# Rolling the rows of a matrix: the head columns loaded as four whole pieces per partition, with the row ends passed on inside SBUF

## The chip, the cores and the metric

The kernel runs on one core of a Trainium2 chip. The core has compute engines, of which this kernel uses two: VectorE (DVE in the profile) for copies inside the on-chip memory SBUF, and GpSimd (POOL), here only to issue DMAs. Two more, SyncE (SP) and ScalarE (ACT), also only issue DMAs. All DMAs of a core are executed by the same 16 DMA engines, whichever engine issued them; the profile calls SP's queue q1 or q10, ACT's the other of these, and POOL's q0. SBUF has 128 partitions. The big arrays lie in DRAM (HBM).

The metric is device time in microseconds; lower is better. Before the change three runs gave 816.09, 816.27 and 818.35 us, median 816.27.

## The reference

```python
def reference(x, shift):           # x: 8192 x 8192 float32, shift: 100
    return np.roll(x, shift, axis=1)
```

Each row is rotated by 100 columns: `out[r, 100:] = x[r, :8092]` and `out[r, :100] = x[r, 8092:]`. Nothing is calculated; 268 MB are read and 268 MB are written. A row is 32 KB.

## The kernel before

The work is cut by columns at `a = 256`. With `s = 100` (the shift) and `g = a - s = 156`:

- **The body**, columns 256 to 8191 of the output, is a plain copy from DRAM to DRAM with the columns shifted by 100. It is issued from SP and ACT (lines 34 to 46), SP going through the rows from the top and ACT from the bottom. One DMA takes 16 rows (every fourth of 64), 496 KB, so each DMA engine has one row of 31 KB; the last two blocks of each side are cut in two by columns. That is 264 DMAs from each of SP and ACT. The name of the last DMA of each block is kept in `marks`.
- **The head**, columns 0 to 255 of the output, goes through SBUF and is issued from POOL. The rows are taken in 16 stages of 512 rows; in a stage each of the 128 partitions has four consecutive rows, q = 0 to 3. A stage has a tile `t` into which DRAM is read and a tile `h` of 128 x 4 x 256 which is written out by one DMA of 512 KB (line 94).

What makes the head cheap to read is that the array is contiguous: the 256 elements that start 100 before the start of row r are the wrapped end of row r-1 (100 elements) followed by the first 156 elements of row r. Such a run of 1 KB is called a piece here. Its first 100 elements belong in the output's row r-1, its last 156 in row r. Before the change a stage reads three pieces per partition, those that start rows q = 1, 2 and 3 (line 85). They give the ends for rows 0, 1, 2 and the starts for rows 1, 2, 3. The two parts that are left, the end of row 3 (400 B per partition, line 86) and the start of row 0 (624 B per partition, line 89), are read straight into `h`. VectorE copies the other parts from `t` to `h` (lines 87 and 90).

What sets the order: POOL works through its instructions in order, first the 48 reads of all stages, then the 16 writes. The helper `fetch` (lines 72 to 78) makes each read wait for the read four before it, so at most four are under way. Write k waits for one of the body's DMAs, chosen by `marks` so that the writes are spread from 3/8 to 15/16 of the body (lines 92 to 97). There are as many `t` and `h` tiles as stages, so no buffer is reused. Dependencies between tiles (a copy after the read of its tile, a write after all that fills its tile) become waits automatically.

Of the kernel before, what the change touches and what calls it, by code (L numbers as in the profile page):

```python
# [1 line left out]

# [4 lines left out]


@with_exitstack
def kernel(  # L10
    ctx: ExitStack,
    tc: tile.TileContext,
    x: bass.AP,
    shift: int,
    out: bass.AP,
):
    nc = tc.nc
    n_rows, n_cols = x.shape
    s = shift % n_cols
    a = -(-s // 128) * 128  # L20
    if 0 < a <= 384 and a + 128 <= n_cols:
        a += 128
    g = a - s
    P = nc.NUM_PARTITIONS
    engines = [nc.sync, nc.scalar]
    n_chunks = 16
    rows = n_rows // n_chunks

    xm = x.rearrange("(c e j) w -> c j e w", e=16, j=4)
    om = out.rearrange("(c e j) w -> c j e w", e=16, j=4)
    marks = []
    if a < n_cols:
        blocks = n_rows // 64
        mid = (a + n_cols) // 256 * 128
        for i in range(blocks // 2):  # L40
            parts = ((a, mid), (mid, n_cols)) if i >= blocks // 2 - 2 and a < mid else ((a, n_cols),)
            for j in range(4):
                for eng, c, q in ((engines[0], i, j), (engines[1], blocks - 1 - i, 3 - j)):
                    for lo, hi in parts:
                        ins = eng.dma_start(out=om[c, q, :, lo:hi], in_=xm[c, q, :, lo - s:hi - s])  # L45
            marks.append(getattr(ins, "ins", ins).name)
    if a == 0:
        return


    if a > 512:
        for i in range(n_chunks):
            r = slice(i * rows, (i + 1) * rows)
            nc.gpsimd.dma_start(out=out[r, :s], in_=x[r, n_cols - s:])
            if g > 0:
                nc.gpsimd.dma_start(out=out[r, s:a], in_=x[r, :g])
        return

    Q = 4
    n_st = n_rows // (P * Q)
    reads = ctx.enter_context(tc.tile_pool(name="reads", bufs=n_st))
    heads = ctx.enter_context(tc.tile_pool(name="heads", bufs=n_st))
    xt = x.rearrange("(k p q) c -> k p q c", q=Q, p=P)
    ot = out.rearrange("(k p q) c -> k p q c", q=Q, p=P)
    tiles = []
    chain = []  # L70

    def fetch(to, of):
        ins = nc.gpsimd.dma_start(out=to, in_=of, single_packet=True)  # L73
        ins = getattr(ins, "ins", ins)
        if len(chain) >= 4:
            tc.add_manual_dep(ins, chain[-4].name,
                              mybir.DependencyInfo(mybir.DependencyClass.Sync, mybir.DependencyReason.DATA))
        chain.append(ins)

    for k in range(n_st):  # L80
        t = reads.tile([P, Q - 1, a], x.dtype)
        h = heads.tile([P, Q, a], x.dtype)
        lead = bass.AP(tensor=x.tensor, offset=(k * P * Q + 1) * n_cols - s,
                       ap=[[Q * n_cols, P], [n_cols, Q - 1], [1, a]])
        fetch(t[:], lead)
        fetch(h[:, Q - 1, :s], xt[k, :, Q - 1, n_cols - s:])
        nc.vector.tensor_copy(h[:, :Q - 1, :s], t[:, :, :s])  # L87
        if g > 0:
            fetch(h[:, 0, s:], xt[k, :, 0, :g])
            nc.vector.tensor_copy(h[:, 1:, s:], t[:, :, s:])  # L90
        tiles.append(h)
    first, last = len(marks) * 3 // 8, len(marks) * 15 // 16
    for k, h in enumerate(tiles):
        ins = nc.gpsimd.dma_start(out=ot[k, :, :, :a], in_=h[:], single_packet=True)  # L94
        if marks and n_st > 1:
            tc.add_manual_dep(getattr(ins, "ins", ins), marks[first + (last - first) * k // (n_st - 1)],
                              mybir.DependencyInfo(mybir.DependencyClass.Sync, mybir.DependencyReason.DATA))


# [1 line left out]
_INS = ['x', 'shift']  # L101
_OUTS = [((8192, 8192), 'float32')]

_NUMBERS = {'shift': 100}


# [26 lines left out]
```

## Time and profile before

| what | value |
|---|---|
| median of three runs | 816.27 us |
| the profiled execution's own time | 816.2 us |
| its span | 814.4 us |
| DVE busy | 12.0 us, 32 instructions |
| POOL busy | 41.2 us, 68 instructions |
| bytes moved by the DMA engines | 276.90 MB, 340 GB/s |
| HBM read / written | 268.44 MB / 268.44 MB, 659 GB/s together |
| median from issue to landing: read of `t` | 29.5 us |
| the two small reads into `h` (78 KB, 50 KB) | 24.3 us, 21.2 us |
| the write of `h` | 21.1 us |
| a body DMA of 496 KB | 12.7 us |

A byte copied from DRAM to DRAM counts once in the bytes moved and twice in the HBM traffic. The share of a DMA queue is the time that its packets took, as a part of the time of all 16 DMA engines. A packet is the unit in which the profile records what one DMA engine does for one queue; small packets include the completion record that each DMA leaves on each engine.

### The profile page before, as it was taken

The numbers are of one execution on the slowest core, as the hardware profiler recorded it, in microseconds if no ns is written. First come the engines' busy times: TensorE is split into PE (matmuls) and PEld (weight loads), VectorE is DVE, ScalarE is ACT, GpSimd is POOL, SyncE is SP. The second block draws the span as 40 slices with busy tenths as digits, with TensorE's granted clock in tenths as the row PEclk, the third lists the DMA queues.
The fourth block names the chain that finished last, engine by engine and source line by source line (L and its number), as shares of the span: only waits on it lengthen the run. The fifth ranks groups of instructions, "written<-read, shape, count | busy, mean of one in ns | idle before, by whom it ended". The sixth has DMA issues, their size and how long they took to land.

```text
span 814.4 us, 689 instructions
## 1 busy us (share of the span) xinstructions
DVE 12.0 (1%) x32; POOL 41.2 (5%) x68
## 2 busy tenths in 40 slices
DVE  0000000000000000000000000000000000000000
POOL 1001001101001000000000000000000000000000
DMA  9999999999999999999999999999999999999998
GB/s 314 346 347 343 351 344 332 338 347 342 356 344 349 345 334 338 345 337 342 337 350 322 352 338 335 357 342 331 352 352 318 356 347 335 340 339 347 334 331 294
DMA packets 22277, 276.90 MB, mean 340 GB/s; under 512 B 9472, under 2 KB 9728, under 8 KB 13824
## 3 DMA queue, kind: packets, MB, share of 16 engines
q1 hardware_dynamic: 8448, 130.04, 46.8%
q10 hardware_dynamic: 8448, 130.04, 44.1%
q0 software_dynamic: 5376, 16.78, 8.1%
q14 instruction: 5, 0.04, 0.0%
HBM read 268.44 MB, written 268.44 MB: 659 GB/s over the span
## 4 chain that ended last, share of the span: by engine, by line
DMA 95%; ACTq 0%; issue 0%; POOLq 0%
DMA out_dram<-in_x_dram 95%; ACTq L45 0%; POOLq L128 0%; POOLq L94 0%
## 5 line engine op out<-in xcount | busy, mean ns | idle before, releaser
L94 POOL DMA_DIRECT2D out_dram<-h x16 | 11.4, 715 | 486.7 <-DMA out_dram<-in_x_dram 448.9
L73 POOL DMA_DIRECT2D h<-in_x_dram x32 | 17.5, 547 | 197.1 <-DMA t<-in_x_dram 165.0
L73 POOL DMA_DIRECT2D t<-in_x_dram x16 | 12.1, 759 | 54.9 <-DMA h<-in_x_dram 54.0
L87 DVE COPY h<-t 128x300 f32<-128x300 f32 x16 | 5.9, 367 | 287.3 <-DMA t<-in_x_dram 287.3
L90 DVE COPY h<-t 128x468 f32<-128x468 f32 x16 | 7.5, 468 | 0.0
L114 POOL MEMSET const-float32-0.0<- 128x1 f32 x1 | 0.1, 99 | 0.2 <-issue 0.2
L114 POOL MEMSET const-bfloat16-1.0<- 128x1 bf16 x1 | 0.1, 102 | 0.0
L114 POOL MEMSET const-float32-1.0<- 128x1 f32 x1 | 0.1, 99 | 0.0
L114 POOL MEMSET const-uint8-127<- 128x1 uint8 x1 | 0.1, 99 | 0.0
## 6 DMA issues: line engine op xcount, KB each, us to landing
out_dram<-in_x_dram SPq DMA_DIRECT2D x248, 496.0 KB, 12.7
out_dram<-in_x_dram ACTq DMA_DIRECT2D x248, 496.0 KB, 12.7
out_dram<-h POOLq DMA_DIRECT2D x16, 512.0 KB, 21.1
t<-in_x_dram POOLq DMA_DIRECT2D x16, 384.0 KB, 29.5
out_dram<-in_x_dram SPq DMA_DIRECT2D x16, 248.0 KB, 5.9
out_dram<-in_x_dram ACTq DMA_DIRECT2D x16, 248.0 KB, 5.9
h<-in_x_dram POOLq DMA_DIRECT2D x16, 78.0 KB, 24.3
h<-in_x_dram POOLq DMA_DIRECT2D x16, 50.0 KB, 21.2
```

Source lines behind the costliest of these rows:

```text
L73: ins = nc.gpsimd.dma_start(out=to, in_=of, single_packet=True)
L87: nc.vector.tensor_copy(h[:, :Q - 1, :s], t[:, :, :s])
L90: nc.vector.tensor_copy(h[:, 1:, s:], t[:, :, s:])
L94: ins = nc.gpsimd.dma_start(out=ot[k, :, :, :a], in_=h[:], single_packet=True)
L114: nc = _bacc.Bacc("TRN2", target_bir_lowering=False, num_devices=1)
```

## The change

A stage now reads all four pieces per partition, those that start rows q = 0 to 3, by one DMA of 512 KB into a tile `t` of 128 x 4 x 256. That gives the ends for rows 0, 1, 2 and the starts of all four rows. The piece q = 0 of partition p+1 begins with the end of row 3 of partition p, so the missing ends are handed over inside SBUF: `pass_on` copies the first 100 elements of piece 0 from partitions 1 to 127 of `t` to partitions 0 to 126 of `h` by a DMA (127 x 400 B), and reads the one end that is left, that of the last partition, from DRAM (400 B). `pass_on` for stage k-2 is issued after the read of stage k, and the last two behind the loop.

In stage 0 the first piece would begin 100 elements before the array, so this stage's read is cut into three: the start of row 0 (1 partition, 624 B), the three other pieces of partition 0 (3 KB), and the four pieces of partitions 1 to 127 (508 KB). All of these go through the same `fetch`, so the rule of four under way holds for them too: 50 fetches in place of 48. VectorE's second copy now takes four rows of 156 elements in place of three. The writes and the body are as before.

```diff
@@ -77,18 +76,35 @@
+    def pieces(row, p, q):
+        return bass.AP(tensor=x.tensor, offset=row * n_cols - s, ap=[[Q * n_cols, p], [n_cols, q], [1, a]])
+
+    tiles, stages = [], []
+
+    def pass_on(k):
+        t, h = stages[k]
+        fetch(h[:P - 1, Q - 1, :s], t[1:, 0, :s])
+        fetch(h[P - 1:, Q - 1, :s], xt[k, P - 1:, Q - 1, n_cols - s:])
+
     for k in range(n_st):
-        t = reads.tile([P, Q - 1, a], x.dtype)
+        t = reads.tile([P, Q, a], x.dtype)
         h = heads.tile([P, Q, a], x.dtype)
-        lead = bass.AP(tensor=x.tensor, offset=(k * P * Q + 1) * n_cols - s,
-                       ap=[[Q * n_cols, P], [n_cols, Q - 1], [1, a]])
-        fetch(t[:], lead)
-        fetch(h[:, Q - 1, :s], xt[k, :, Q - 1, n_cols - s:])
-        nc.vector.tensor_copy(h[:, :Q - 1, :s], t[:, :, :s])
+        if k == 0:
+            if g > 0:
+                fetch(t[:1, 0, s:], xt[0, :1, 0, :g])
+            fetch(t[:1, 1:, :], pieces(1, 1, Q - 1))
+            fetch(t[1:], pieces(Q, P - 1, Q))
+        else:
+            fetch(t[:], pieces(k * P * Q, P, Q))
+        nc.vector.tensor_copy(h[:, :Q - 1, :s], t[:, 1:, :s])
         if g > 0:
-            fetch(h[:, 0, s:], xt[k, :, 0, :g])
-            nc.vector.tensor_copy(h[:, 1:, s:], t[:, :, s:])
+            nc.vector.tensor_copy(h[:, :, s:], t[:, :, s:])
         tiles.append(h)
+        stages.append((t, h))
+        if k >= 2:
+            pass_on(k - 2)
+    for k in range(max(n_st - 2, 0), n_st):
+        pass_on(k)
```

More of the change, by code (lines that the diff above doesn't have):

```diff
@@ L68 @@
     ot = out.rearrange("(k p q) c -> k p q c", q=Q, p=P)
-    tiles = []
     chain = []
```

## The prediction

> **What bounds the kernel now.** I read the page's parts 2 to 5 first, then the DMA view in windows for the three kinds of stretch that the kernel has, then POOL's timeline around the switch from reads to writes.
>
> The page says at once that no compute engine matters:
>
> ```profile
> span 814.4 us, 689 instructions
> DVE 12.0 (1%) x32; POOL 41.2 (5%) x68
> DMA packets 22277, 276.90 MB, mean 340 GB/s; under 512 B 9472, under 2 KB 9728, under 8 KB 13824
> q1 hardware_dynamic: 8448, 130.04, 46.8%
> q10 hardware_dynamic: 8448, 130.04, 44.1%
> q0 software_dynamic: 5376, 16.78, 8.1%
> HBM read 268.44 MB, written 268.44 MB: 659 GB/s over the span
> DMA 95%; ACTq 0%; issue 0%; POOLq 0%
> ```
>
> The three queues' shares add up to 99%: the 16 DMA engines always have a packet in hand, and the chain that ends last is the body's DMAs, 95% of the span. The head's queue q0 is 8.1% of the engines' time for 6.1% of the bytes.
>
> Is it the engines or the memory that is full? The DMA view answers in three stretches. Reads and body, 20 to 270 us (first three lines); writes and body, 400 to 760 us (next three); body nearly alone, 610 to 630 us (last two):
>
> ```profile
> q1 hardware_dynamic: 2485, 39.46, 44.3%
> q10 hardware_dynamic: 2477, 39.21, 39.6%
> q0 software_dynamic: 2731, 7.38, 15.4%
> ...
> q1 hardware_dynamic: 3673, 58.26, 48.3%
> q10 hardware_dynamic: 3676, 58.48, 47.2%
> q0 software_dynamic: 1722, 6.29, 4.6%
> ...
> q1 hardware_dynamic: 204, 3.40, 52.8%
> q10 hardware_dynamic: 207, 3.17, 48.7%
> ```
>
> Bytes moved: 344, 342 and 329 GB/s. HBM traffic, with the body's bytes counted twice and q0's once: (2 x 78.67 + 7.38) / 250 us = 659 GB/s; (2 x 116.74 + 6.29) / 360 us = 666; 2 x 6.57 / 20 us = 657. The second set is within 1.4%, the first within 4.6%, and a body packet moves faster where the head loads HBM less: 78.67 MB in 83.9% of 16 x 250 us is 23.4 GB/s per engine, alone it is 20.2. So HBM traffic is nearer to the limit than the engines, though the engines show no gap. A q0 packet takes 15.4% x 250 / (2731 / 16) = 0.226 us in the read stretch, and 4.6% x 360 / (1722 / 16) = 0.154 us in the write stretch.
>
> POOL's timeline from the last stage's reads to the first write:
>
> ```profile
> 278.82 0.56 POOL L73 DMA_DIRECT2D h<-in_x_dram  x1 [8.61 <-DMA t<-in_x_dram]
> 281.45 0.54 POOL L73 DMA_DIRECT2D h<-in_x_dram  x1 [2.07 <-DMA h<-in_x_dram]
> 327.69 0.73 POOL L94 DMA_DIRECT2D out_dram<-h  x1 [45.70 <-DMA out_dram<-in_x_dram]
> ```
>
> Reading a stage takes (281.45 - 2.17) / 15 = 18.6 us, the reads are all issued by 281.5 us and landed some 24 us later, and POOL then waits for the body until 327.7. There is a cover of about 22 us.
>
> **The change part by part.** The sum is made against the profiled execution, 816.2 us (span 814.4 and 1.8 around it); the median of the three runs is 816.27.
>
> *HBM traffic.* A stage read 384 + 50 + 78 = 512 KB from DRAM; now it reads 512 KB and 400 B. In stage 0 the first piece's 400 B fall away. 16 x 400 - 400 = 6 KB more of 537 MB: nothing, 0.01 us at 659 GB/s.
>
> *Bytes on the DMA engines.* New are 127 x 400 B per stage from SBUF to SBUF, 0.81 MB in all. If the engines are the limit, at 340 GB/s, that is 2.4 us; if HBM is, 0.
>
> *Packets on the DMA engines.* q0 has 5376 / 16 stages / 16 engines = 21 packets per stage and engine. Four are completion records (9472 small packets are 16 x 64 from POOL's DMAs and 16 x 528 from the body's). The other 17 fit pieces of at most 4 KB: 24 KB of `t` in 6, 3.1 KB of ends in 1, 4.9 KB of starts in 2 (the 256 packets between 512 B and 2 KB are their remainders), 32 KB written in 8. Afterwards, if 127 partitions are shared out 8 to an engine: 8 + 1 for `t`, 1 + 1 for the hand-over, 1 completion for the single end, 8 + 1 for the write: again 21. One packet per stage now reads SBUF in place of HBM; priced as a packet of the write stretch it would save 0.226 - 0.154 = 0.07 us, 1.2 us over 16 stages, were the engines the limit. So this part lies between -1.2 and +2.4. I take the middle, +0.6: the 340 GB/s row is a full-engine row, the equal HBM traffic speaks for less.
>
> *Small packets under HBM load.* The read stretch's dearer packet (0.226 against 0.154) includes the pieces of 400 and 624 B. The Trainium skill, "DMA: Bandwidth & Descriptors", section "Why small descriptors are slow (HBM only)", says that the penalty of small pieces belongs to HBM and that transfers within SBUF don't suffer it. The rows agree in direction only; by the rule the hand-over sits at the lower end, -1.2, and the sum would be 815.0 instead.
>
> *POOL and its waits.* 50 fetches for 48. The two added in stage 0 and the heavier `t` cost POOL some 2 x 0.55 us of issue; it is busy 5%. What each fetch waits for keeps its pattern: the hand-over's first DMA finds the fetch of `t` of the next-but-one stage ahead of it and waits for the `t` four places back; the next waits for a hand-over, `t` for a single end. The hand-over also waits for its own `t`, which is six places back and landed. So a stage stays near 18.6 us (12 read packets per engine before and after), and two more fetches of three per stage are 12 us: last issue at about 294 us, landed by about 318, the first write due at 327.7. Cover left: about 10 us. If it is gone, the writes queue behind the reads in POOL's order; write k is due some 30 us after the one before, up to 779 us, and a write is issued in 0.71 us, so a delay of even 150 us is caught up before the last is due. Price at the end: 0. SP's and ACT's queues get nothing new and are not moved past.
>
> *VectorE.* The second copy grows from 468 to 624 elements: 367 ns for 300 and 468 ns for 468 give 0.6 ns per element, so about 562 ns, 16 x 94 ns = 1.5 us more on an engine 1% busy, with the copies under the next read's wait: 0.
>
> Sum: 816.2 + 0.6 = 816.8 us; 815.0 to 818.6 by the bounds.
>
> **The rivals.**
>
> *Slower: 127 partitions land on one DMA engine.* Nothing in the trace shows how a transfer of 127 is shared out: every DMA before has 128 partitions or 16 rows, both divisible by 16. Bounded from the other side, all of it goes to one engine. For stage 0 that is 508 KB in 127 packets on an engine whose even part is 32 KB: 476 KB too much. At one engine's part of 340 GB/s, 21.25 GB/s, it is 22.4 us, and as every body DMA needs all 16 engines with about four under way per queue (12.7 us to land), the other engines soon wait for that one: 838 us. If the idle engines leave their HBM share to it (23.4 GB/s against 20.2 shows that a packet speeds up by 16% when HBM has less to do), it catches most up: nearly 816. Between them: about 828. The hand-overs, 50.8 KB on one engine in turn, add up to 48 KB / 21.25 GB/s = 2.2 us where an engine is hit, partly evened out between engines. It decides as soon as the split is uneven by more than 50 KB (2.4 us) on some engine. For it: 127 is prime. Against: POOL's own program builds these transfers and needs no equal parts. The Trainium skill, "DMA: Bandwidth & Descriptors", section "Why a DMA increments its semaphore by 16 and not by 1", gives the largest count up to 16 that divides the partitions, which for 127 is 1, and beside it an exception for some direct copies from GpSimd, 8 partitions per engine, 127 on all 16. By the rule the time is this rival's, by the exception it is the forecast's; no run here shows which.
>
> *Slower in a smaller way: the hand-over moves at q0's rate in the read stretch.* 7.38 MB in 15.4% of 16 x 250 us is 12 GB/s per engine; 50.8 KB more per engine at that rate is 4.2 us, with no relief from HBM: 820.4. For it: shares that fill the engines. Against: equal packet counts.
>
> *Faster: the small reads were what made q0 dear.* If the 9 packets per stage of `t` and completions cost 0.154 us as in the write stretch, the 12 at 0.226 leave (2.71 - 1.39) / 3 = 0.44 us for each of the three small ones, and twelve packets at 0.154 save 0.86 us per stage, 13.8 us on every engine: 802 if the engines are the limit, and nothing if HBM is. With HBM traffic equal within 1.4%, a sixth to a half of it at most: about 811.
>
> That the change doesn't do what it says has no place here: the DMAs are plain.
>
> **How the numbers follow.** 0.3%, 2.4 us, is about what a measurement of this kernel can tell from no change. Forecast, even split: 0.50, about 816.8, its own range 814.5 to 819; one engine: 0.32, 818 to 838, most likely 828; the hand-over at 12 GB/s: 0.09; faster: 0.09. Nearly all of the forecast (0.44) lies within 813.8 to 818.7, with 0.02 below and 0.04 above; the one-engine case gives 0.03 to "same". So faster 0.11, same 0.47, slower 0.42. The range leaves out the faster case below 813.5 and the upper third of the one-engine case: 813.5 to 832.
>
> **What would show it.** Even split: the 508 KB read of stage 0 lands after about 30 us like the other reads, the reads are all issued by about 294 us, the first write near 328, q0 about 8% with some 5,430 packets and 17.6 MB, 277.7 MB in all, HBM still 537 MB. One engine: that read takes over 150 us to land (127 packets at the 1.55 us between q0 packets of one engine, 18.6 us / 12), POOL sits behind it, and the mean DMA share falls below 0.95 in that stretch or at the end. Hand-over dear: q0 above 8.6%. Faster: the read stretch above 350 GB/s and q0 below 7.5%. The prediction is wrong first of all if the split is uneven, and then by the size of what HBM gives back.

## The result and the profile after

The changed kernel takes 818.75 us (median of 17 runs) against 816.18 us for the kernel before on the same chips: a ratio of 1.0033, 95% interval 1.0025 to 1.0041. It is slower by 2.6 us, a small but clear difference by that interval. The profiled execution has a span of 817.5 us, 3.1 more than before.

The page of the changed kernel, parts 1, 3, 4 and 6. A line of a queue (q) has its packets, their MB and the share; a line of part 6 ends with the size of one issue and the median time from issue to landing:

```profile
span 817.5 us, 693 instructions
DVE 12.1 (1%) x32; POOL 47.0 (6%) x70
DMA packets 24501, 277.75 MB, mean 340 GB/s; under 512 B 11694, under 2 KB 11697, under 8 KB 16048
q10 hardware_dynamic: 8448, 130.04, 46.4%
q1 hardware_dynamic: 8448, 130.04, 43.9%
q0 software_dynamic: 7600, 17.63, 8.3%
HBM read 268.44 MB, written 268.44 MB: 657 GB/s over the span
DMA 95%; ACTq 0%; issue 0%; POOLq 0%
...
t<-in_x_dram POOLq DMA_DIRECT2D x15, 512.0 KB, 35.9
h<-t POOLq DMA_DIRECT2D x16, 49.6 KB, 23.2
t<-in_x_dram POOLq DMA_DIRECT2D x1, 508.0 KB, 215.5
```

The bound is the same: the queues' shares sum to 98.6%, HBM traffic is unchanged, and the chain is the body's DMAs. Two lines are new. Stage 0's read of 127 partitions took 215.5 us to land where its fifteen siblings took 35.9. And q0 has 7,600 packets, where I expected some 5,430. The 2,222 small ones beyond those of before are mostly one kind: the trace's packet records show 1,905 of 16 bytes between 11 and 54 us, which is 15 x 127, and 127 packets of 4,096 bytes that follow each other some 1.6 us apart up to 218 us. (The other small ones are completions, the single ends, each in ten packets of 40 bytes, and the start of row 0 in 13 of 48.) A record doesn't name its engine, but the reading that fits both counts is that one engine carries all the data of this read, and each of the other 15 goes through 127 tiny packets. The hand-overs are shared out: their records are 240 packets of 3,200 bytes (15 engines x 16 stages, eight runs of 400) and 16 of 2,804 (the last engine's seven and 4 bytes more).

POOL's timeline of the changed kernel shows what hangs on the uneven read. A line has start and duration in us, engine, kernel line, operation, what is moved and how many; in brackets stand the idle time before it and what ended it:

```profile
1.30 7.28 POOL L72 DMA_DIRECT2D t<-in_x_dram  x5 [0.85 <-PEq L144]
218.57 0.56 POOL L72 DMA_DIRECT2D h<-t  x1 [210.00 <-DMA t<-in_x_dram]
...
510.10 0.52 POOL L72 DMA_DIRECT2D h<-in_x_dram  x1 [2.55 <-DMA h<-in_x_dram]
510.69 3.73 POOL L110 DMA_DIRECT2D out_dram<-h  x5
```

POOL issues five reads and then sits for 210 us until stage 0 has landed. The last fetch is issued at 510 us in place of 281, and the writes that were due by then go out in a bunch.

So three things could make up the 2.6 us. S: the uneven read by itself, above all the 476 KB too much on one engine. L: the lateness that comes from it, with eight writes bunched between 510 and 527 us. H: the hand-overs' 0.81 MB, 2.4 us at 340 GB/s.

### The profile page after: what moved, and what is told of

Its sections match the earlier page's. It is cut to its first block, busy times and chain, and to the rows that moved or that the text cites. A ratio compares the mean times of both kernels' runs of the same rounds, so it can differ in the third digit from the quotient of the medians.

```text
span 817.5 us, 693 instructions
## 1 busy us (share of the span) xinstructions
DVE 12.1 (1%) x32; POOL 47.0 (6%) x70
## 4 chain that ended last, share of the span: by engine, by line
DMA 95%; issue 0%; ACTq 0%; POOLq 0%
DMA out_dram<-in_x_dram 95%; ACTq L45 0%; POOLq L144 0%; POOLq L110 0%
## 5 line engine op out<-in xcount | busy, mean ns | idle before, releaser
L72 POOL DMA_DIRECT2D h<-t x16 | 9.5, 596 | 394.0 <-DMA t<-in_x_dram 376.8
L72 POOL DMA_DIRECT2D t<-in_x_dram x18 | 17.4, 970 | 37.8 <-DMA h<-in_x_dram 25.4
L72 POOL DMA_DIRECT2D h<-in_x_dram x16 | 8.3, 521 | 43.1 <-DMA h<-t 25.3
L101 DVE COPY h<-t 128x624 f32<-128x624 f32 x16 | 7.5, 470 | 0.0
## 6 DMA issues: line engine op xcount, KB each, us to landing
out_dram<-in_x_dram ACTq DMA_DIRECT2D x248, 496.0 KB, 12.6
out_dram<-in_x_dram SPq DMA_DIRECT2D x248, 496.0 KB, 12.6
t<-in_x_dram POOLq DMA_DIRECT2D x15, 512.0 KB, 35.9
t<-in_x_dram POOLq DMA_DIRECT2D x1, 508.0 KB, 215.5
```

The costliest lines, as they stand in the source:

```text
L101: nc.vector.tensor_copy(h[:, :, s:], t[:, :, s:])
```

## The experiments

**1. Stage 0 read evenly.** The changed kernel with the 127 partitions cut into 112 and 15:

```diff
-            fetch(t[1:], pieces(Q, P - 1, Q))
+            fetch(t[1:113], pieces(Q, 112, Q))
+            fetch(t[113:], pieces(113 * Q, P - 113, Q))
```

> The changed kernel with stage 0's read of 127 partitions cut into 112 and 15 partitions, which 16 and 15 engines can share evenly; all else, hand-overs included, as changed. Three theories of the +2.6 us of the changed kernel (818.75 against 816.18): S, the 476 KB too much on one DMA engine; L, the lateness that follows from it (all reads issued by 511 us in place of 282, eight writes bunched between 510 and 527 us); H, the 0.81 MB of hand-overs, 2.4 us at 340 GB/s. S and L both expect this kernel at 816.2 to 816.7, with stage 0's read landed by about 40 us and the first write near 328 us. H expects 818.6 to 818.8.

Measured: 816.22 us (12 runs), 816.58 for the kernel before beside it, ratio 1.0002 (0.9994 to 1.0011). Its page, part 6, and POOL's timeline:

```profile
t<-in_x_dram POOLq DMA_DIRECT2D x1, 448.0 KB, 22.4
```
```profile
336.08 0.76 POOL L111 DMA_DIRECT2D out_dram<-h  x1
```

The 448 KB land in 22.4 us, the first write goes out at 336 us (8 us later than expected), and the loss is gone, with all sixteen hand-overs in place. H falls. S or L remains.

**2. The uneven read alone.** The kernel before, with only stage 0 read and handed over as in the changed kernel:

```diff
     for k in range(n_st):
+        if k == 0:
+            fetch(t[:1, 0, s:], xt[0, :1, 0, :g])
+            fetch(t[:1, 1:, :], pieces(1, 1, Q - 1))
+            fetch(t[1:], pieces(Q, P - 1, Q))
...
+            continue
...
```

> The kernel before, with stage 0 alone read and handed over as in the changed kernel (508 KB in one DMA of 127 partitions); the other 15 stages as before, so one hand-over in place of 16. S and L expect 818.6 to 818.9, with stage 0's read landing after 200 us or more. H expects 816.3 (a sixteenth of 2.4 us more).

Measured: 819.04 us (12 runs), ratio 1.0031 (1.0021 to 1.0041). POOL's timeline has the same wait:

```profile
214.08 0.81 POOL L73 DMA_DIRECT2D t<-in_x_dram  x1 [206.18 <-DMA t<-in_x_dram]
```

The one transfer brings back the whole loss, with one hand-over instead of sixteen.

**3. Lateness alone.** The kernel before, with its first four reads made to wait for the body:

```diff
         if len(chain) >= 4:
             tc.add_manual_dep(ins, chain[-4].name, ...)
+        else:
+            tc.add_manual_dep(ins, marks[16], ...)
```

> The kernel before, with its first four reads held back until the body's 17th block (about 215 us), so that the reads run from about 218 to 505 us and the writes bunch as in the changed kernel; no DMA is uneven and nothing is handed over. L expects 818.6 to 818.9. S and H expect 816.2.

Measured: 816.22 us (12 runs), ratio 1.0006 (0.9993 to 1.0018). POOL's timeline of this kernel:

```profile
214.00 0.88 POOL L73 DMA_DIRECT2D t<-in_x_dram  x1 [213.55 <-DMA out_dram<-in_x_dram]
...
489.32 2.95 POOL L97 DMA_DIRECT2D out_dram<-h  x4
```

The reads start at 214 us and the writes bunch at 489 us, nearly as in the changed kernel, and it costs at most 1.5 us by the interval, 0.5 by its middle. L falls as the main cause. S stands, by these runs for the uneven transfer as a whole: its tiny packets come and go with its large ones.

**4. Hand-overs three and a half times as large.** The kernel before, with extra copies inside SBUF that nothing reads:

```diff
...
+        if k >= 2:
+            over = spare.tile([P, 400], x.dtype)
+            nc.gpsimd.dma_start(out=over[:P - 1, :], in_=stages[k - 2][1:, :400], single_packet=True)
```

> The kernel before, with 14 extra DMAs inside SBUF of 127 partitions x 1,600 B into a tile that nothing reads: 2.84 MB, 3.5 times the changed kernel's hand-overs, not counted among the four reads under way. H (bytes priced at the engines' 340 GB/s) expects 816.2 + 8.4 = 824.6. S and L expect 816.2 to 816.8, since HBM has nothing more to move.

Measured: 817.43 us (12 runs), ratio 1.0014 (1.0002 to 1.0026): 1.1 us (0.2 to 2.1) for 2.84 MB, where the engines' 340 GB/s would ask 8.4. Scaled to the changed kernel's 0.81 MB that is 0.3 us, and part of it may be the later reads (the median landing of `t` rose to 43.2 us). Bytes that stay inside SBUF cost about a seventh of the engines' price here, and by the interval at most a quarter.

**5. Two uneven reads.** Experiment 1's kernel, with stages 1 and 2 each cut into 1 and 127 partitions:

```diff
+        elif k <= 2:
+            fetch(t[:1], pieces(k * P * Q, 1, Q))
+            fetch(t[1:], pieces(k * P * Q + Q, P - 1, Q))
```

> The first experiment's kernel (even stage 0), with stages 1 and 2 each read as 1 and 127 partitions: two transfers of 508 KB that each go to one engine, both under way at once. If they land on different engines they take some 215 us side by side, on the same engine some 430 us one after the other. Theory A, the cost is a fixed toll per uneven transfer (2.5 us each, 817.4 to 819 for one): 821.2. Theory B, the cost is set by the engine with most to do: on different engines 818.7 as for one, on the same engine 821.2 or more.

Measured: 820.53 us (6 runs), ratio 1.0062 (1.0040 to 1.0084), near what theory A expects, and theory B if both reads are on the same engine. In the profiled execution, the slowest of the six at 826.74 us, the two landed one after the other: the second did not land until 433 us, the last read was issued at 679 us, and POOL's timeline shows the writes crowded up to the end:

```profile
679.88 3.73 POOL L114 DMA_DIRECT2D out_dram<-h  x5
...
797.86 0.71 POOL L114 DMA_DIRECT2D out_dram<-h  x1 [4.91 <-issue]
```

So the run mixes the uneven reads with their lateness, and experiment 9 was made to part them.

**6 and 7. An uneven read late, and its even twin.** Experiment 1's kernel with the last stage's read placed behind write 6, once as 1 + 127 partitions (shown), once as 1 + 112 + 15:

```diff
...
+        if k == 6:
+            k = n_st - 1
+            fetch(t[:1], pieces(k * P * Q, 1, Q))
+            fetch(t[1:], pieces(k * P * Q + Q, P - 1, Q))
...
```

> The first experiment's kernel with the last stage read as 1 and 127 partitions and issued only after write 6, near 504 us, so that the uneven transfer runs from about 505 to 720 us and little of the body is left behind it. Theory C, HBM gives the time back during the transfer itself (the other 15 engines wait and the loaded one speeds up): 818.7 as in the changed kernel. Theory D, the loaded engine falls behind by up to 22 us and catches up in the 600 us that follow: with 95 us left, well over 821, towards 835.

> The same as the uneven late read, but cut into 1, 112 and 15 partitions, so that nothing is uneven: what the moved order costs by itself. All theories expect 816.2 to 816.8; the difference of the two late kernels is the price of the unevenness late in the run.

Measured: uneven 818.49 us (12 runs), ratio 1.0033 (1.0016 to 1.0049); even 817.24 us (12 runs), 1.0009 (0.9999 to 1.0020). The order did not come out as meant: the read was moved ahead of the writes in POOL's instructions and was issued at 310 us, to land at 518, so 300 us of the body were left and not 95. As a test of theory D it is weaker than planned. Nor is the twin its equal in all else: its writes go out from 328 us on at their usual times, while those of the uneven kernel wait for the read and start at 519 us, seven at once. Between the two lie 0.24% or 2.0 us, and with the intervals of both some 0.4 to 3.5 us; the two profiled executions differ by nothing (spans of 813.8 and 813.9 us). So a toll of the same size in the middle of the run as at its start is possible by these runs, and not shown; a cost of 20 us is excluded (the interval of the uneven kernel ends at 0.49%, 4 us).

**8. Stage 0 by four DMAs of one run per partition.**

```diff
-            fetch(t[1:], pieces(Q, P - 1, Q))
+            for q in range(Q):
+                one = bass.AP(tensor=x.tensor, offset=(Q + q) * n_cols - s, ap=[[Q * n_cols, P - 1], [1, a]])
+                fetch(t[1:, q, :], one)
```

> The changed kernel with stage 0's 127 partitions read by four DMAs of 127 x 1 KB, one per row of the four, in place of one of 127 x 4 KB. If any transfer from DRAM of 127 partitions goes to one engine, the four take some 215 us in all, or 55 us each on engines in turn, and the time stays above 816.8. If the shape of 127 single runs is what lets a transfer be shared (as the 127 runs of a hand-over are, which landed in 23 us), they land in 20 to 30 us each and the time is 816.2 to 816.8.

Measured: 816.75 us (10 runs), ratio 1.0009 (0.9999 to 1.0019). Part 6 of its page:

```profile
t<-in_x_dram POOLq DMA_DIRECT2D x4, 127.0 KB, 18.3
```

The same 127 partitions and the same bytes land in 18.3 us: 127 is not the trouble by itself. The interval includes no change, so without the single-engine read the loss is gone again.

**9. Reads held back further.** Experiment 3 with `marks[32]` in place of `marks[16]`:

> The kernel before, with its first four reads held back until the body's 33rd block (about 408 us), so that the reads end near 700 us and the writes crowd into the last 120 us, as in the kernel with two uneven transfers, with nothing uneven. If two uneven transfers are two tolls of 2 to 2.5 us (theory A), this kernel is at 816.2 to 817. If the 820.5 us of that kernel came from the crowding, this one is at 819 to 821.

Measured, on a slower chip: 830.61 us (6 runs) against 826.59 for the kernel before beside it, ratio 1.0047 (1.0033 to 1.0060). With nothing uneven, writes crowded into the last 133 us cost 0.47%. That is most of experiment 5's 0.62%, and the intervals overlap, so experiment 5 does not show two tolls. Whether two uneven transfers cost twice one stays open.

**10. One run of 4 KB per partition.** The kernel before with one more read, issued first:

```diff
+    spare = ctx.enter_context(tc.tile_pool(name="spare", bufs=1))
+    over = spare.tile([P, 1024], x.dtype)
+    nc.gpsimd.dma_start(out=over[1:, :], in_=x[1:P, :1024], single_packet=True)
```

> The kernel before with one more read, issued first, of 127 partitions x 4 KB, each partition's 4 KB being one contiguous run of a row (508 KB in all, into a tile that nothing reads). If the 4 KB per partition put the changed kernel's read on one engine, this one also takes 200 us to land; if the four separate runs per partition did, it is shared over 16 engines and lands in 15 to 30 us.

It was timed once (828.41 us, on the chip of experiment 9), so only its landing is used. Its DMA, in the view of its tile:

```profile
L82 POOL DMA_DIRECT2D over<-in_x_dram x1: 668/668/668, 1.3 to 1.3; - x1
...
DMA to landing us min/median/max: 15.8/15.8/15.8
```

508 KB to 127 partitions in 15.8 us, with 17 more packets of 4 bytes than before, 127 more of 4,096 and none of 16: shared out. So neither 127 nor the 4 KB per partition put the changed kernel's read on one engine, but the four runs per partition in one DMA. Why that shape is treated otherwise no run shows.

## Where the 22 us went

Against the rival's 22.4 us, of which I took 12, measured were 2.4 (0.31% of experiment 2 less 0.02% of experiment 1). The right kernel to compare the traces with is experiment 3's, which has nearly the same schedule with nothing uneven. The DMA view from 20 to 215 us, first of the changed kernel, then of experiment 3:

```profile
q10 hardware_dynamic: 2006, 31.84, 50.1%
q1 hardware_dynamic: 1994, 31.46, 43.9%
q0 software_dynamic: 2224, 1.51, 4.1%
...
out_dram<-in_x_dram ACTq DMA_DIRECT2D x62, 496.0 KB, 12.6
```
```profile
q1 hardware_dynamic: 2050, 32.54, 50.8%
q10 hardware_dynamic: 2045, 32.38, 48.6%
...
out_dram<-in_x_dram ACTq DMA_DIRECT2D x63, 496.0 KB, 12.4
```

Had 15 engines waited for the loaded one throughout, some 11% of this stretch (22.4 of 195 us) would be idle. The shares sum to 98.1% against 99.4%: 1.3%, 2.5 us. HBM traffic was 2 x 63.30 + 1.51 = 128.1 MB against 129.8, and 1.7 MB at 657 GB/s are 2.6 us. A body DMA, which needs all 16 engines, lands in 12.6 us against 12.4: the loaded engine is not falling behind by 22 us. The landing records say the same: from the first to the last of the 16 engines of one body DMA it is 7.4 us in the mean and 9.9 at most (30 to 210 us of the changed kernel); in experiment 3, 5.4 and 8.3; in the kernel before, 7.0 and 10.4. So against experiment 3 the loaded engine is some 2 us behind, and the time is given back while the read runs, not in the 600 us behind it (theory C, not D).

Could the tiny packets be the loss? Their records take 10.7 ns each, 1.4 us on each of the 15 engines, and they are over at 54 us. From 20 to 60 us the shares sum to 100.3% in both kernels, and HBM traffic is 26.3 MB against 26.6, which is worth 0.5 us. From 60 to 215 us, again first the changed kernel:

```profile
q10 hardware_dynamic: 1602, 25.49, 51.3%
q1 hardware_dynamic: 1588, 25.05, 43.9%
q0 software_dynamic: 196, 0.73, 2.3%
...
q1 hardware_dynamic: 1625, 25.81, 50.7%
q10 hardware_dynamic: 1626, 25.81, 48.5%
```

The shares sum to 97.5% against 99.2%, 2.6 us, and HBM traffic is 101.8 MB against 103.2, 2.2 us; experiment 2 has 97.0% and 102.6 MB. So most of the loss lies where the tiny packets are over and the large ones go on. No run has the tiny packets alone.

How the loaded engine keeps up can be read from the packet records. Its body packets can be picked out by following packets that start within 4 ns of another's end, from one q0 packet to the next (the shortest such chain, as the records have no engine). Between 80 and 205 us they took 1.35 us in the mean (73 packets) where all engines' took 1.48; in experiment 2, 1.27 (78 packets) against 1.47. The fastest body packets of any engine take 1.17 us, the fastest q0 packets of 4,096 bytes 0.16, and 35 of the changed kernel's 78 steps from one q0 packet to the next take just the sum, 1.33: one packet of each queue, both at their best. So a packet has some room below its usual time, and the loaded engine gets it. That this is because the other engines leave it their HBM share is the likely reason, not one that a run isolates. The before-after sums of single profiled executions have a spread of about 1 us, so the 2.2 to 2.6 us above are pointers; the timed ratios of experiments 1 and 2 carry the verdict.

## Why the prediction was right and where it was wrong

- **The time** of 818.75 us lies inside the range (816.8, 813.5 to 832.0), but on the side of the rival: slower by 2.6 us, where the likeliest case was no measurable change. That owes something to luck. The sum has no term for an uneven read; it held where none is (816.22 in experiment 1, 816.75 in experiment 8), and the kernel as changed came out near it because the rival cost 2.4 us and not the 12 that were taken.
- **The step that failed** is "if 127 partitions are shared out 8 to an engine". It held for the hand-overs and failed for the one read of stage 0, which took 215.5 us to land with 127 packets on one engine. I had treated "127 partitions" as one question; the trace of before had no such transfer, and I gave the split one chance for all of them. Experiments 8 and 10 show that it goes by shape: one run per partition was shared, four runs per partition in one DMA were not. The Trainium skill, "DMA: Bandwidth & Descriptors", section "Why a DMA increments its semaphore by 16 and not by 1", has both the rule (127 goes to one engine) and the exception (8 per engine); both happened in one kernel.
- **The rival's size** failed too: about 828 was taken, 818.75 measured. Its lower end, "nearly 816", was close to right. The 16% between body packets in two stretches was in the text as a row (23.4 against 20.2 GB/s per engine), and I took the middle of the two ends without a reason in place of following it: an engine that needs 11% more time in a stretch and whose packets can go 16% faster can nearly keep pace. The row was misread, though: HBM traffic was the same in both stretches (659 and 657 GB/s), so HBM had not "less to do" there; the body had a smaller part of it. (The 22.4 us also count a KB as 1,000 bytes; with the profile's 1,024 they are 22.9.)
- **How it would show**: landing over 150 us, from 127 packets at 1.55 us, was right (215.5), and so was POOL behind it. A mean DMA share below 0.95 in that stretch was wrong: it was 0.98.
- **HBM traffic +6 KB, 0.01 us**: right, 657 GB/s against 659 only because the span is longer.
- **The hand-over's bytes**, -1.2 to +2.4, +0.6 taken: experiment 1 with all of them is at +0.2 us (-0.5 to +0.9), experiment 4 gives 0.3 (0.1 to 0.6). The small price was right; the engines' 2.4 lies outside both. "The hand-over moves at q0's rate", 4.2 us: refuted by the same two runs.
- **"Faster: the small reads were what made q0 dear"**: refuted. Experiment 1 has the whole pieces and no gain.
- **A late POOL costs nothing, because the last write is due at 779 us**: right within the noise for the delay that came (last fetch 229 us later than before in the changed kernel, 207 us later in experiment 3, which cost 0.06%, -0.07 to 0.18). It has an end: by experiment 9, reads that last until 700 us cost 0.47%.
- **The cover of about 10 us for the reads**: in the even kernel the last fetch was issued at 335.5 us and not 294, past the first write's 327.7; each stage took 20.8 us and not 18.6, with `t` landing in 35.5 us. The cover was gone, and the price was 0 as stated.
- **POOL's issues**: 1.1 us more were expected, 5.8 came (41.2 to 47.0 us busy), most of it one issue (below). It cost nothing that a run shows by itself.

## What to carry to other kernels

Before an edge case is split off a 128-partition DMA, look at what shape the odd part has: 127 partitions with four runs each went through a single engine here, while 112 + 15 partitions, or one DMA per run, were shared. The landing time of each issue, not the mean DMA share, is where this shows: 215 us beside 36, with the share still at 0.98. And an extra load on one engine need not cost its bytes at that engine's mean rate: here it cost about a ninth of that. Read from the trace how much faster a packet can go at best before pricing it.

## What the runs showed of the hardware that was not expected

- A read of 127 partitions x 4 runs of 1 KB put 127 packets of 4,096 B on one engine and 127 packets of 16 B on each of the other 15.
- POOL was busy for 4.6 us with issuing such a read (4.61 in the changed kernel, 4.56 to 4.60 in experiments 5 and 6), where one of 512 KB on 128 partitions took 0.78: the shape shows already at the issue.
- VectorE's copy of 128 x 624 elements took no longer than that of 128 x 468, where I had expected 562 ns from the slope between 300 and 468. The groups of the changed kernel:

```profile
L99 DVE COPY h<-t 128x300 f32<-128x300 f32 x16 | 5.9, 368 | 493.0 <-DMA t<-in_x_dram 493.0
L101 DVE COPY h<-t 128x624 f32<-128x624 f32 x16 | 7.5, 470 | 0.0
```
